# Loading 16 rows of each of eight batches per tile, and scanning during the loads

## The chip, the cores and the metric

The kernel runs on one core of a Trainium2 chip. The metric is device time in microseconds (us), as the median of several executions. The profile is one execution taken by the hardware profiler; its span is about 1.7 us shorter than the measured time (645.1 against 646.76 for the kernel before). "DVE" is VectorE, "PE" TensorE, "ACT" ScalarE, "POOL" GpSimd, "SP" the engine that issues loads. x lies in HBM, the large memory; a load brings it to SBUF, the on-chip memory of 128 partitions; PSUM is where PE leaves its results. "16 engines" in the queue tables are the core's DMA engines, as the page counts them.

## The reference

```
# x: 8 x 2048 x 4096 float32 (268 MB), w: 4096 x 1
proj = (x @ w).squeeze(-1)                      # 8 x 2048
cm = np.maximum.accumulate(proj, axis=1)
is_record = (proj >= cm).astype(np.float32)
return np.cumsum(is_record, axis=1)
```

All of x is read once. The arithmetic is one multiply and one add per element, and then two prefix operations over 2048 values in each of 8 batches.

## The kernel before

x is taken as 16384 rows. Tile t is 128 neighbouring rows, one row (16 KB) to each partition; a load is one uniform step of a row per partition. DVE multiplies by w and sums in one instruction. The last tile is shared between DVE and POOL plus ACT. The results, 128 rows by 128 tiles, are transposed, and then two chains of seven shifted steps compute the prefix maximum and the prefix sum inside blocks of 128, with small matrix work to join the blocks.

```python
x_tiled = x_flat.rearrange("(t v) d -> t v d", v=P)      # P = 128
xpool = ctx.enter_context(tc.tile_pool(name="xpool", bufs=8))
# ... w broadcast to 128 partitions through PE ...
for t in range(NT):                                       # NT = 128
    x_sb = xpool.tile([P, D], FP32)                       # D = 4096
    nc.sync.dma_start(out=x_sb, in_=x_tiled[t])
    # ... (t == NT - 1: POOL multiply and ACT sum of the last 1280 columns) ...
    nc.vector.scalar_tensor_tensor(out=x_sb, in0=x_sb, scalar=1.0, in1=w_bcast,
        op0=mult, op1=mult, accum_out=proj_all[:, t:t + 1])
# ... transpose, two chains of 7 shifted steps, joining of blocks, output ...
```

## Time and profile before

| what | value | where read |
|---|---|---|
| time | 646.76 us (646.76 to 647.03, 3 runs) | executions |
| load rate in the middle | 428 to 435 GB/s | slices of the page |
| load queue | 97.4% of the 16 engines | queue table |
| DVE per tile | starts 4.85 us apart, 4.35 when work is waiting | timeline |
| after the last load | 16.6 us of 645.1 | timeline |

From the page of the kernel before, the busy share of the DMA engines (in tenths) and the rate in 40 equal slices, and the load queue (packets, MB, share of 16 engines):

```profile
DMA  8999999999999999999999999999999999999980
GB/s 350 430 435 429 433 430 432 429 435 428 434 428 433 432 431 431 433 432 430 432 430 434 429 433 429 433 430 432 433 430 434 430 432 429 433 429 435 428 344 4
...
q1 hardware_dynamic: 18578, 268.53, 97.4%
```

The rate is nearly constant from the second slice to the last but two. The timeline of DVE near the end (start, duration, engine, line, operation, and in brackets the idle time before it and what ended it):

```profile
604.27 4.43 DVE L146 SCALAR_TENSOR_TENSOR x_sb<-x_sb,w_bcast 128x4096 f32<-128x4096 f32 x1 [0.42 <-DMA x_sb<-in_x_dram]
...
609.12 4.42 DVE L146 SCALAR_TENSOR_TENSOR x_sb<-x_sb,w_bcast 128x4096 f32<-128x4096 f32 x1 [0.42 <-DMA x_sb<-in_x_dram]
```

Each multiply-reduce waits 0.4 us for its load: starts are 4.85 us apart, and that is the pace of the loads, not of DVE. The group of these instructions on the page (busy us, mean ns, idle before and most of its cause):

```profile
L146 DVE SCALAR_TENSOR_TENSOR x_sb<-x_sb,w_bcast 128x4096 f32<-128x4096 f32 x127 | 560.5, 4425 | 65.7 <-DMA x_sb<-in_x_dram 47.5
```

What this kernel does once the last tile has landed, from its timeline:

```profile
628.56 3.09 DVE L131 SCALAR_TENSOR_TENSOR x_sb<-x_sb,w_bcast 128x2816 f32<-128x2816 f32 x1 [0.41 <-DMA x_sb<-in_x_dram]
628.63 5.75 POOL L120 TENSOR_TENSOR x_sb<-x_sb,w_bcast 128x1280 f32<-128x1280 f32 x1 [624.11 <-DMA x_sb<-in_x_dram]
...
634.42 1.27 ACT L125 ACTIVATE x_sb<-x_sb 128x1280 f32<-128x1280 f32 x1 [615.29 <-POOL x_sb L120]
...
637.01 0.29 DVE L186 TENSOR_TENSOR bufB<-bufA 128x128 f32<-128x128 f32 x1
...
642.34 0.29 DVE L238 TENSOR_SCALAR final<-bufD,ps_ps 128x128 f32<-128x128 f32 x1
642.66 0.35 SPq L243 DMA_DIRECT2D out_dram<-final  x1
```

The last load lands at about 628.5. POOL then takes 5.75 us for its share of the tile, ACT follows, and the chains of shifted steps run from 637 (the first is shown) to 642.6. A faster tail is worth what it takes off these 16.6 us; a faster DVE in the middle is worth nothing.

### The profile page before, as it was taken

To read this page: it belongs to the slowest core of one execution; us is meant where nothing else is said; L and a number is where in the kernel's file an instruction comes from. 1 tells how busy PE (TensorE), PEld (TensorE's weight loads), DVE (VectorE), ACT (ScalarE), POOL (GpSimd) and SP (SyncE) were. 2 spreads that over 40 slices of the span, in tenths; PEclk is the share of its full clock that TensorE was granted. 3 is DMA by queue.
4 is the path that set the end of the run, shared out by engine and by line. 5 is a ranking of instruction groups with operands and counts; after the bars stand their busy time and mean duration, and the time that the engine had idled before them with its cause. 6 is when DMAs were issued, how large, how long until landed. Compare 5 with 4: busy or idle time off the path is not lost.

```text
span 645.1 us, 776 instructions
## 1 busy us (share of the span) xinstructions
PE 15.5 (2%) x20; PEld 6.0 (1%) x20; DVE 570.0 (88%) x279; ACT 6.4 (1%) x5; POOL 9.5 (1%) x21
## 2 busy tenths in 40 slices
PE   7000000000000000000000000000000000000000
PEld 3000000000000000000000000000000000000000
DVE  0899999898998998998989899899899898989984
ACT  1100000000000000000000000000000000000000
POOL 2000000000000000000000000000000000000003
DMA  8999999999999999999999999999999999999980
GB/s 350 430 435 429 433 430 432 429 435 428 434 428 433 432 431 431 433 432 430 432 430 434 429 433 429 433 430 432 433 430 434 430 432 429 433 429 435 428 344 4
DMA packets 18583, 268.57 MB, mean 416 GB/s; under 512 B 2065, under 2 KB 2193, under 8 KB 2193
## 3 DMA queue, kind: packets, MB, share of 16 engines
q1 hardware_dynamic: 18578, 268.53, 97.4%
q14 instruction: 5, 0.04, 0.0%
HBM read 268.45 MB, written 0.07 MB: 416 GB/s over the span
## 4 chain that ended last, share of the span: by engine, by line
DMA 75%; DVE 18%; issue 3%; PE 2%; POOLq 1%; ACT 0%; DVEq 0%; ACTq 0%
DMA x_sb<-in_x_dram 74%; DVE x_sb L146 17%; PE psum_wb L55 2%; POOLq L269 1%; DMA w_bcast<-in_w_dram 0%; ACT w_bcast L62 0%; ACT x_sb L125 0%; DVE bufD L227 0%; DVE bufB L186 0%; DVE bufC L227 0%; DVE bufA L186 0%; PE ps_t L168 0%; DVE bufC L206 0%; DVE bufA L171 0%; DVE final L238 0%
## 5 line engine op out<-in xcount | busy, mean ns | idle before, releaser
L146 DVE SCALAR_TENSOR_TENSOR x_sb<-x_sb,w_bcast 128x4096 f32<-128x4096 f32 x127 | 560.5, 4425 | 65.7 <-DMA x_sb<-in_x_dram 47.5
L168 PE MATMUL ps_t<-identity,proj_all 128*128 128x128 f32 x1 | 0.4, 447 | 618.9 <-DVE proj_all L140 618.9
L120 POOL TENSOR_TENSOR x_sb<-x_sb,w_bcast 128x1280 f32<-128x1280 f32 x1 | 5.8, 5755 | 624.1 <-DMA x_sb<-in_x_dram 624.1
L55 PE MATMUL psum_wb<-w_bcast,ones_70 1*128 1x512 f32 x16 | 14.0, 1064 | 3.2 <-DMA w_bcast<-in_w_dram 3.2
L146 DVE DVE_READ_ACCUMULATOR x_sb<-x_sb,w_bcast 128x1 f32 x127 | 10.5, 83 | 0.0
L125 ACT ACTIVATE x_sb<-x_sb 128x1280 f32<-128x1280 f32 x1 | 1.3, 1269 | 615.3 <-POOL x_sb L120 615.3
L168 PEld LDWEIGHTS ps_t<-identity,proj_all 128*128 128x128 f32 x1 | 0.2, 182 | 620.4 <-issue 620.4
L55 PEld LDWEIGHTS psum_wb<-w_bcast,ones_70 1*128 1x128 f32 x16 | 5.2, 330 | 10.5 <-issue 10.5
L140 DVE TENSOR_TENSOR proj_all<-proj_all,aux_109 128x1 f32<-128x1 f32 x1 | 0.2, 160 | 4.2 <-ACT x_sb L125 4.2
L131 DVE SCALAR_TENSOR_TENSOR x_sb<-x_sb,w_bcast 128x2816 f32<-128x2816 f32 x1 | 3.1, 3093 | 0.4 <-DMA x_sb<-in_x_dram 0.4
L61 ACT COPY w_bcast<-psum_wb 128x2048 f32<-128x2048 f32 x1 | 1.9, 1865 | 6.0 <-PE psum_wb L55 6.0
L62 ACT COPY w_bcast<-psum_wb 128x2048 f32<-128x2048 f32 x1 | 1.9, 1865 | 5.0 <-PE psum_wb L55 5.0
L227 DVE TENSOR_TENSOR bufD<-bufC 128x128 f32<-128x128 f32 x4 | 1.2, 292 | 0.2
L186 DVE TENSOR_TENSOR bufB<-bufA 128x128 f32<-128x128 f32 x4 | 1.2, 291 | 0.2
L61 ACT ACT_TABLE_LOAD x1 | 1.3, 1283 | 3.2 <-DMA w_bcast<-in_w_dram 3.2
L186 DVE TENSOR_TENSOR bufA<-bufB 128x128 f32<-128x128 f32 x3 | 0.9, 292 | 0.2
L227 DVE TENSOR_TENSOR bufC<-bufD 128x128 f32<-128x128 f32 x3 | 0.9, 292 | 0.2
L48 DVE MEMSET ones_70<- 1x128 f32 x1 | 0.2, 165 | 0.9 <-PEq L258 0.9
L171 DVE TENSOR_SCALAR_CACHE_REDUCE bufA<-ps_t 128x128 f32<-128x128 f32 x1 | 0.3, 292 | 0.6 <-PE ps_t L168 0.6
L217 PE MATMUL ps_ps<-blocksum,msum 128*128 128x1 f32 x2 | 0.6, 348 | 2.5 <-DVE bufC L206 2.5
L217 PEld LDWEIGHTS ps_ps<-blocksum,msum 128*128 128x128 f32 x2 | 0.5, 310 | 2.8 <-issue 2.8
L177 PE MATMUL ps_bm<-identity,blockmax 128*128 128x128 f32 x1 | 0.5, 473 | 0.4 <-DVE bufA L171 0.4
(29 smaller groups left out, 6.2 us busy)
## 6 DMA issues: line engine op xcount, KB each, us to landing
x_sb<-in_x_dram SPq DMA_DIRECT2D x128, 2048.0 KB, 34.3
out_dram<-final SPq DMA_DIRECT2D x1, 64.0 KB, 1.5
w_bcast<-in_w_dram SPq DMA_DIRECT2D x1, 16.0 KB
```

Source lines behind the costliest of these rows:

```text
L55: nc.tensor.matmul(out=psum_wb[:, a * 512:(a + 1) * 512], lhsT=ones1, rhs=w_bcast[0:1, a * 512:(a + 1) * 512], start=True, stop=True,)
L61: nc.scalar.copy(out=w_bcast[:, :D // 2], in_=psum_wb[:, :D // 2])
L62: nc.scalar.copy(out=w_bcast[:, D // 2:], in_=psum_wb[:, D // 2:])
L120: nc.gpsimd.tensor_mul(out=x_sb[:, FV:], in0=x_sb[:, FV:], in1=w_bcast[:, FV:],)
L125: nc.scalar.activation(out=x_sb[:, FV:], in_=x_sb[:, FV:], func=mybir.ActivationFunctionType.Copy, accum_out=aux127,)
L131: nc.vector.scalar_tensor_tensor(out=x_sb[:, :FV], in0=x_sb[:, :FV], scalar=1.0, in1=w_bcast[:, :FV], op0=mybir.AluOpType.mult, op1=mybir. ...
L146: nc.vector.scalar_tensor_tensor(out=x_sb, in0=x_sb, scalar=1.0, in1=w_bcast, op0=mybir.AluOpType.mult, op1=mybir.AluOpType.mult, accum_ou ...
L168: nc.tensor.transpose(out=ps_t, in_=proj_all, identity=identity)
L186: nc.vector.tensor_tensor(out=nxt[:, PAD:], in0=cur[:, PAD:], in1=cur[:, PAD - k:W - k], op=mybir.AluOpType.max,)
L217: nc.tensor.matmul(out=ps_ps, lhsT=msum, rhs=blocksum, start=True, stop=True,)
L227: nc.vector.tensor_tensor(out=nxt[:, PAD:], in0=cur[:, PAD:], in1=cur[:, PAD - k:W - k], op=mybir.AluOpType.add,)
L269: with _tile.TileContext(nc) as tc:
```

## The change

Its intent is to bring every batch forward at the same time, 16 rows of each batch per tile, so that the prefix scans can run during the loads, and to have little left at the end. Partition j*8+b holds row j of batch b. For three quarters of the rows a partition takes two neighbouring rows (32 KB). A matmul with 0/1 entries turns 128 results per tile into 8 rows, one for each batch; two scans, chained from group to group, replace the chains of shifted steps. The last tiles are cut into column pieces on DVE.

```diff
-    x_tiled = x_flat.rearrange("(t v) d -> t v d", v=P)
+    NJ = P // B          # 16 rows of each of 8 batches
+    STEP = NJ
+    LONG = 2             # rows per partition, for the first three quarters
+    PIECES = {NT - 4: (0, 4096), NT - 3: (0, 2304, 4096),
+              NT - 2: (0, 2048, 4096), NT - 1: (0, 1920, 4096 - 512, 4096)}
-    xpool = ctx.enter_context(tc.tile_pool(name="xpool", bufs=8))
+    xpool = ctx.enter_context(tc.tile_pool(name="xpool", bufs=5))    # 32 KB each
+    def x_rows(t, r, c0, c1):
+        return bass.AP(
+            tensor=x.tensor,
+            offset=x.offset + t * STEP * D + c0,
+            ap=[[r * D, NJ], [S * D, B], [1, (r - 1) * D + c1 - c0]],
+        )
...
-        nc.sync.dma_start(out=x_sb, in_=x_tiled[t])
+        nc.sync.dma_start(
+            out=x_sb[:, : (r - 1) * D + c1 - c0], in_=x_rows(t, r, c0, c1)
+        )
...
+            nc.scalar.activation(out=dst, in_=is_j, func=ACTF.Copy, scale=acc)
...
+            nc.tensor.matmul(out=ps[:, : n * STEP], lhsT=is_b,
+                             rhs=rhs[:, : n * STEP], start=True, stop=True)
...
+        nc.vector.tensor_tensor_scan(out=cm[:, :N], data0=ps[:, :N], ...)
+        nc.vector.tensor_tensor(out=rec[:, :N], in0=ps[:, :N], in1=cm[:, :N], op=ALU.is_ge)
+        nc.vector.tensor_tensor_scan(out=cnt[:, :N], data0=rec[:, :N], ...)
...
-    # POOL/ACT share of the last tile, transposes, two chains of 7 shifted steps
```

`ap=[[r * D, NJ], [S * D, B], ...]`: the source of a load now has 16 groups of 8 partitions. Two batches lie S*D floats, 32 MiB, apart.

More of the change, by code (lines that the diff above doesn't have):

```diff
@@ L13 @@
 FP32 = mybir.dt.float32
-NEG_BIG = -1.0e30
+ALU = mybir.AluOpType
+ACTF = mybir.ActivationFunctionType
+NEG = -3.0e38
 @with_exitstack
@@ L28 @@
     B, S, D = x.shape
-    R = B * S
-    NT = R // P
-    assert NT == P
-    x_flat = x.flatten_outer_dims()
-    x_tiled = x_flat.rearrange("(t v) d -> t v d", v=P)
-    out_flat = bass.AP(tensor=out.tensor, offset=out.offset,
-                       ap=[[P, NT], [1, P]])
-    const_pool = ctx.enter_context(tc.tile_pool(name="const", bufs=1))
-    xpool = ctx.enter_context(tc.tile_pool(name="xpool", bufs=8))
-    ppool = ctx.enter_context(tc.tile_pool(name="ppool", bufs=1))
+    NJ = P // B
@@ new lines @@
+    STEP = NJ
+    NT = S // STEP
+    LONG = 2
+    LONG_UNTIL = NT - 32
+    PIECES = {
+        NT - 4: (0, 4096),
+        NT - 3: (0, 2304, 4096),
+        NT - 2: (0, 2048, 4096),
+        NT - 1: (0, 1920, 4096 - 512, 4096),
+    }
+    GROUP = 16
+    LASTG = 4
+    const_pool = ctx.enter_context(tc.tile_pool(name="const", bufs=1))
+    xpool = ctx.enter_context(tc.tile_pool(name="xpool", bufs=5))
+    gpool = ctx.enter_context(tc.tile_pool(name="gpool", bufs=2))
+    def x_rows(t, r, c0, c1):
[4 more added lines that the diff above has]
+        )
@@ new lines, with start_load @@
+    loads = []
+    for t in range(0, LONG_UNTIL, LONG):
+        loads.append((t, LONG, 0, D))
+    for t in range(LONG_UNTIL, NT):
+        cuts = PIECES.get(t, (0, D))
+        for c0, c1 in zip(cuts[:-1], cuts[1:]):
+            loads.append((t, 1, c0, c1))
+    def start_load(i):
+        t, r, c0, c1 = loads[i]
+        x_sb = xpool.tile([P, LONG * D], FP32, name="x_sb")
+        nc.sync.dma_start(
+            out=x_sb[:, : (r - 1) * D + c1 - c0], in_=x_rows(t, r, c0, c1)
+        )
+        return x_sb
@@ new lines @@
+    first = [start_load(i) for i in range(2)]
+    w_bcast = const_pool.tile([P, D], FP32)
+    w_row = w_bcast[0:1, :]
+    nc.scalar.dma_start(out=w_row, in_=w.rearrange("d one -> one d"))
+    ones1 = const_pool.tile([1, P], FP32)
+    nc.vector.memset(ones1, 1.0)
+    with tc.tile_pool(name="wbpsum", bufs=1, space=bass.MemoryType.PSUM) as wbpool:
+        psum_wb = wbpool.tile([P, D], FP32)
+        for a in range(D // 512):
+            cols = slice(a * 512, (a + 1) * 512)
+            nc.tensor.matmul(
+                out=psum_wb[:, cols], lhsT=ones1, rhs=w_row[:, cols],
+                start=True, stop=True,
+            )
+        nc.scalar.copy(out=w_bcast[:, : D // 2], in_=psum_wb[:, : D // 2])
+        nc.scalar.copy(out=w_bcast[:, D // 2 :], in_=psum_wb[:, D // 2 :])
@@ L43 @@
+    psum_pool = ctx.enter_context(
+        tc.tile_pool(name="psum", bufs=2, space=bass.MemoryType.PSUM)
+    )
     identity = const_pool.tile([P, P], FP32)
     make_identity(nc, identity)
-    w_bcast = const_pool.tile([P, D], FP32)
-    ones1 = const_pool.tile([1, P], FP32)
-    nc.vector.memset(ones1, 1.0)
-    nc.sync.dma_start(out=w_bcast[0:1, :], in_=w.rearrange("d one -> one d"))
-    with tc.tile_pool(name="wbpsum", bufs=1, space=bass.MemoryType.PSUM) as wbpool:
-        psum_wb = wbpool.tile([P, D], FP32)
-        NCH = D // 512
-        for a in range(NCH):
+    is_b = const_pool.tile([P, B], FP32)
@@ new lines @@
+    is_j = const_pool.tile([P, NJ], FP32)
+    neg = const_pool.tile([B, GROUP * STEP], FP32)
+    zero = const_pool.tile([B, GROUP * STEP], FP32)
+    nc.gpsimd.memset(neg, NEG)
+    nc.gpsimd.memset(zero, 0.0)
+    nc.vector.reduce_sum(
+        out=is_b, in_=identity.rearrange("p (j b) -> p b j", b=B),
+        axis=mybir.AxisListType.X,
+    )
+    nc.vector.reduce_sum(
+        out=is_j, in_=identity.rearrange("p (j b) -> p j b", b=B),
+        axis=mybir.AxisListType.X,
+    )
+    proj = const_pool.tile([P, NT], FP32)
@@ new lines, with scan_group @@
+    parts = const_pool.tile([P, 32], FP32)
+    groups = []
+    t = 0
+    while t < NT:
+        n = GROUP if t + GROUP <= NT - LASTG else (NT - LASTG - t if t < NT - LASTG else LASTG)
+        groups.append((t, n))
+        t += n
+    state = {"cm": None, "cnt": None}
+    def scan_group(t0, n, ps):
+        N = n * STEP
+        cm = gpool.tile([B, GROUP * STEP], FP32, name="cm")
+        rec = gpool.tile([B, GROUP * STEP], FP32, name="rec")
+        cnt = gpool.tile([B, GROUP * STEP], FP32, name="cnt")
+        nc.vector.tensor_tensor_scan(
+            out=cm[:, :N], data0=ps[:, :N], data1=neg[:, :N],
+            initial=NEG if state["cm"] is None else state["cm"],
+            op0=ALU.max, op1=ALU.max,
+        )
+        nc.vector.tensor_tensor(
+            out=rec[:, :N], in0=ps[:, :N], in1=cm[:, :N], op=ALU.is_ge
+        )
+        nc.vector.tensor_tensor_scan(
+            out=cnt[:, :N], data0=rec[:, :N], data1=zero[:, :N],
+            initial=0.0 if state["cnt"] is None else state["cnt"],
+            op0=ALU.add, op1=ALU.add,
+        )
+        state["cm"] = cm[:, N - 1 : N]
+        state["cnt"] = cnt[:, N - 1 : N]
+        eng = nc.sync if t0 + n == NT else nc.scalar
+        eng.dma_start(
+            out=bass.AP(
+                tensor=out.tensor, offset=out.offset + t0 * STEP,
+                ap=[[S, B], [1, N]],
+            ),
+            in_=cnt[:, :N],
+        )
@@ new lines @@
+    pending = None
+    gi = 0
+    rhs = None
+    npart = 0
+    for i, (t, r, c0, c1) in enumerate(loads):
+        x_sb = first[i] if i < 2 else start_load(i)
+        t0, n = groups[gi]
+        if c0 == 0 and t == t0:
+            rhs = gpool.tile([P, GROUP * STEP], FP32, name="rhs")
+        for q in range(r):
+            if c0 == 0 and c1 == D:
+                acc = proj[:, t + q : t + q + 1]
+            else:
+                acc = parts[:, npart : npart + 1]
+                npart += 1
+            xs = x_sb[:, q * D : q * D + c1 - c0]
+            nc.vector.scalar_tensor_tensor(
+                out=xs, in0=xs, scalar=1.0,
+                in1=w_bcast[:, c0:c1], op0=ALU.mult, op1=ALU.mult, accum_out=acc,
+            )
+            base = (t - t0) * STEP
+            dst = rhs[:, base : base + r * STEP].rearrange("p (j q) -> p q j", q=r)[:, q]
+            if c0 == 0:
+                nc.scalar.activation(out=dst, in_=is_j, func=ACTF.Copy, scale=acc)
+            else:
+                nc.vector.scalar_tensor_tensor(
+                    out=dst, in0=is_j, scalar=acc, in1=dst, op0=ALU.mult, op1=ALU.add
+                )
+        if pending is not None and (t + r - 1 >= pending[0] + pending[1] + 1):
+            scan_group(*pending)
+            pending = None
+        if c1 == D and t + r == t0 + n:
+            ps = psum_pool.tile([B, GROUP * STEP], FP32, name="ps")
@@ L55 @@
             nc.tensor.matmul(
-                out=psum_wb[:, a * 512:(a + 1) * 512],
-                lhsT=ones1,
-                rhs=w_bcast[0:1, a * 512:(a + 1) * 512],
+                out=ps[:, : n * STEP], lhsT=is_b, rhs=rhs[:, : n * STEP],
                 start=True, stop=True,
             )
-        nc.scalar.copy(out=w_bcast[:, :D // 2], in_=psum_wb[:, :D // 2])
-        nc.scalar.copy(out=w_bcast[:, D // 2:], in_=psum_wb[:, D // 2:])
-    psum_pool = ctx.enter_context(tc.tile_pool(name="psum", bufs=1, space=bass.MemoryType.PSUM))
@@ L66 @@
-    GB = 16
-    NGB = P // GB
-    blockdiag = const_pool.tile([P, P], FP32)
-    nc.gpsimd.memset(blockdiag, 0.0)
-    nc.gpsimd.affine_select(
-        out=blockdiag, in_=blockdiag,
-        compare_op=mybir.AluOpType.is_gt,
-        fill=1.0, base=1 - GB,
-        pattern=[[-GB, NGB], [0, GB]], channel_multiplier=1,
-    )
-    nc.gpsimd.affine_select(
-        out=blockdiag, in_=blockdiag,
-        compare_op=mybir.AluOpType.is_ge,
-        fill=0.0, base=0,
-        pattern=[[-GB, NGB], [0, GB]], channel_multiplier=1,
-    )
@@ L84 @@
-    strict_lt_col = const_pool.tile([P, P], FP32)
-    nc.gpsimd.memset(strict_lt_col, 1.0)
-    nc.gpsimd.affine_select(
-        out=strict_lt_col, in_=strict_lt_col,
-        compare_op=mybir.AluOpType.is_ge,
-        fill=0.0, base=-1,
-        pattern=[[-1, P]], channel_multiplier=1,
-    )
-    strict_gt_col = const_pool.tile([P, P], FP32)
-    nc.gpsimd.memset(strict_gt_col, 1.0)
-    nc.gpsimd.affine_select(
-        out=strict_gt_col, in_=strict_gt_col,
-        compare_op=mybir.AluOpType.is_ge,
-        fill=0.0, base=-1,
-        pattern=[[1, P]], channel_multiplier=-1,
-    )
@@ L102 @@
-    maxmask = const_pool.tile([P, P], FP32)
-    nc.gpsimd.tensor_mul(out=maxmask, in0=blockdiag, in1=strict_lt_col)
-    nc.gpsimd.tensor_scalar(
-        out=maxmask, in0=maxmask, scalar1=-1.0, scalar2=-NEG_BIG,
-        op0=mybir.AluOpType.add, op1=mybir.AluOpType.mult,
-    )
-    msum = const_pool.tile([P, P], FP32)
-    nc.gpsimd.tensor_mul(out=msum, in0=blockdiag, in1=strict_gt_col)
-    proj_all = const_pool.tile([P, NT], FP32)
-    FV = 2816
-    aux127 = const_pool.tile([P, 1], FP32)
@@ L116 @@
-    for t in range(NT):
-        x_sb = xpool.tile([P, D], FP32)
-        nc.sync.dma_start(out=x_sb, in_=x_tiled[t])
-        if t == NT - 1:
-            nc.gpsimd.tensor_mul(
-                out=x_sb[:, FV:],
-                in0=x_sb[:, FV:],
-                in1=w_bcast[:, FV:],
-            )
-            nc.scalar.activation(
-                out=x_sb[:, FV:],
-                in_=x_sb[:, FV:],
-                func=mybir.ActivationFunctionType.Copy,
-                accum_out=aux127,
-            )
-            nc.vector.scalar_tensor_tensor(
-                out=x_sb[:, :FV],
-                in0=x_sb[:, :FV],
-                scalar=1.0,
-                in1=w_bcast[:, :FV],
-                op0=mybir.AluOpType.mult,
-                op1=mybir.AluOpType.mult,
-                accum_out=proj_all[:, t:t + 1],
-            )
-            nc.vector.tensor_add(
-                out=proj_all[:, t:t + 1],
-                in0=proj_all[:, t:t + 1],
-                in1=aux127,
-            )
-        else:
-            nc.vector.scalar_tensor_tensor(
-                out=x_sb,
-                in0=x_sb,
-                scalar=1.0,
-                in1=w_bcast,
-                op0=mybir.AluOpType.mult,
-                op1=mybir.AluOpType.mult,
-                accum_out=proj_all[:, t:t + 1],
-            )
@@ L156 @@
-    PAD = 64
-    W = PAD + P
-    bufA = ppool.tile([P, W], FP32)
-    bufB = ppool.tile([P, W], FP32)
-    bufC = ppool.tile([P, W], FP32)
-    bufD = ppool.tile([P, W], FP32)
-    nc.gpsimd.memset(bufA[:, :PAD], NEG_BIG)
-    nc.gpsimd.memset(bufB[:, :PAD], NEG_BIG)
-    nc.gpsimd.memset(bufC[:, :PAD], 0.0)
-    nc.gpsimd.memset(bufD[:, :PAD], 0.0)
-    ps_t = psum_pool.tile([P, P], FP32)
-    nc.tensor.transpose(out=ps_t, in_=proj_all, identity=identity)
-    blockmax = const_pool.tile([P, 1], FP32)
@@ L171 @@
-    nc.vector.tensor_scalar(
-        out=bufA[:, PAD:], in0=ps_t, scalar1=1.0, scalar2=None,
-        op0=mybir.AluOpType.mult, op1=mybir.AluOpType.max,
-        accum_out=blockmax,
-    )
-    ps_bm = psum_pool.tile([P, P], FP32)
-    nc.tensor.transpose(
-        out=ps_bm,
-        in_=blockmax.to_broadcast([P, P]),
-        identity=identity,
-    )
-    cur, nxt = bufA, bufB
-    k = 1
-    while k < P:
-        nc.vector.tensor_tensor(
-            out=nxt[:, PAD:],
-            in0=cur[:, PAD:],
-            in1=cur[:, PAD - k:W - k],
-            op=mybir.AluOpType.max,
-        )
-        cur, nxt = nxt, cur
-        k *= 2
@@ L194 @@
-    cm = cur[:, PAD:]
-    masked_bm = ppool.tile([P, P], FP32)
-    prefmax = const_pool.tile([P, 1], FP32)
-    nc.vector.tensor_tensor_reduce(
-        out=masked_bm, in0=ps_bm, in1=maxmask,
-        scale=1.0, scalar=NEG_BIG,
-        op0=mybir.AluOpType.add, op1=mybir.AluOpType.max,
-        accum_out=prefmax,
-    )
-    blocksum = const_pool.tile([P, 1], FP32)
-    nc.vector.scalar_tensor_tensor(
-        out=bufC[:, PAD:],
-        in0=cm,
-        scalar=prefmax,
-        in1=ps_t,
-        op0=mybir.AluOpType.max,
-        op1=mybir.AluOpType.is_le,
-        accum_out=blocksum,
-    )
@@ L216 @@
-    ps_ps = psum_pool.tile([P, 1], FP32)
-    nc.tensor.matmul(
-        out=ps_ps,
-        lhsT=msum,
-        rhs=blocksum,
-        start=True, stop=True,
-    )
-    cur, nxt = bufC, bufD
-    k = 1
-    while k < P:
-        nc.vector.tensor_tensor(
-            out=nxt[:, PAD:],
-            in0=cur[:, PAD:],
-            in1=cur[:, PAD - k:W - k],
-            op=mybir.AluOpType.add,
-        )
-        cur, nxt = nxt, cur
-        k *= 2
-    cs = cur[:, PAD:]
-    final = ppool.tile([P, P], FP32)
@@ L238 @@
-    nc.vector.tensor_scalar(
-        out=final, in0=cs, scalar1=ps_ps, scalar2=None,
-        op0=mybir.AluOpType.add,
-    )
-    nc.sync.dma_start(out=out_flat, in_=final)
+            pending = (t0, n, ps)
+            gi += 1
+    scan_group(*pending)
 _INS = ['x', 'w']
```

## The prediction

> **What bounds the kernel now.** The load stream. The page's slices show 428 to 435 GB/s in all but the first and last two; the queue table gives the load queue 97.4% of the 16 engines. In the timeline VectorE (DVE) multiply-reduce starts are 4.84 to 4.88 us apart, each after a short wait for a load; back to back, behind the late start, 4.35 us. So DVE has 0.49 us of slack per 2 MB tile. After the last landing (about 628.5 us) comes a serial tail to 645.1, 16.6 us: 5.8 POOL multiply, 1.5 ScalarE sum, transposes and fourteen shifted 128x128 steps (636 to 642.6), 2.5 for the output.
>
> **What changes.**
> 1. Loads. Same bytes, 32 KB rows for 96 of 128 tiles. From packet times worked out of the trace (a 16 KB row 611 ns, a 512 B one 27, a semaphore write 9) the fixed part of a row is some ns; halving their number saves about 1.5 us (estimate). The first load no longer queues behind w: 0.4 us. [...]here eight batches lie 32 MiB apart, but the 16 row groups are adjacent, so I expect little loss. No trace here shows it. Last landing: about 626.6.
> 2. DVE gains nine scan groups. [...]against 16 x 0.49 of slack: free, except near the end. The 0/1 matmuls and ScalarE expansions are off the critical path.
> 3. The late start remains (w broadcast on PE, 14 us)[...]. Five 4 MB buffers cover it.
> 4. The tail. POOL, transposes and shift steps go. But the instruction order puts the 192-column scan right after its group's last multiply, so DVE waits there for ScalarE and PE[...]. The last four tiles then cost DVE about 4.35 + 13.4 (seven pieces at 1.04 ns per column + 0.09 us)[...] = 18.9 us, while they land within 14.5. So I expect DVE, not DMA, to end this stage, some 6 us after the last landing, then matmul 0.5[...], output 2.5: about 10 us in place of 16.6.
>
> **Sum.** Stream 1.9 us earlier, tail 6.4 shorter: 8.3 us, nearly all critical. 646.76 - 8.3 = 638.5 us, range 632 to 645. Chances: faster by over 2% 0.17, within 2% 0.75, slower by over 2% 0.08.
>
> **What would show it.** Rate: slices near 432 to 435 GB/s, two-row landings about 9.68 us apart. Tail: in the timeline DVE runs back to back over the pieces, without waits for DMA, from a wait for PE before the 192-column scan; 9 to 11 us from last landing to the end. No wait of the load queue on DVE that leaves the DMA row below 9. If the last pieces wait for DMA instead, DVE was not behind, the tail is 5 us, and the time about 633.
>
> **What would make it wrong.** The new split of rows over DMA engines or the 32 MiB pitch lowers the rate: one per cent is 6 us, a collision far more. Longer rows could gain more than 1.5 us. Scans or semaphore waits on DVE could be longer near the end.

Cut out of it is what no trace of this case shows: in item 1 a statement on distances between rows, in item 2 a speed for scans and two estimates made from it, in item 3 a guess about w, in item 4 three terms that count in scan times. The sums still contain those terms. The first, in item 4, is the wait with scan and comparison; the last four tiles came to 18.9 us on DVE, that is 4.35 + 13.4 and the second; 18.9 less 14.5, plus the first, gives the "some 6 us"; with 0.5, 2.5 and the third the tail came to about 10 us. The stream's 1.9 us are 1.5 + 0.4. The whole came to 8.3 us and so to 638.5 us.

## The result

The changed kernel takes 1282.7 us (median of 4 runs, 1274.2 to 1286.6) against 646.77 us (4 runs). The ratio of the means of the fast runs is 1.98 (95% interval 1.974 to 1.988); ratios here are the mean time of one kernel's fast runs over that of the other's in the same rounds, so not quite the ratio of the quoted medians. The predicted 638.5 us is off by a factor of two.

The same lines of the page of the changed kernel:

```profile
DMA  9999999999999999999999999999999999999997
GB/s 204 208 214 214 214 209 207 211 214 213 210 206 211 214 213 210 203 214 214 208 204 214 213 211 202 214 214 213 210 204 216 220 216 218 216 217 219 215 218 171
...
q1 hardware_dynamic: 12112, 268.44, 99.7%
```

The reader should look at the two rows together. The DMA row reads 9 in all slices but the last, and the queue's share has even risen, from 97.4% to 99.7%; but the rate is 200 to 220 GB/s. The engines are busy all the time and move half as much. The bytes are the same to 0.1%.

The waits of DVE for loads (who waited for what, total us, times, longest us) of the kernel before:

```profile
DVE x_sb L146 <- DMA x_sb<-in_x_dram: 47.5, 106, 1.4
```

The multiply-reduce group on the page of the changed kernel, and then its waits of DVE for loads:

```profile
L172 DVE SCALAR_TENSOR_TENSOR x_sb<-x_sb,w_bcast 128x4096 f32<-128x4096 f32 (+2 forms) x132 | 563.2, 4294 | 676.7 <-DMA x_sb<-in_x_dram 676.7
```

```profile
DVE x_sb L172 <- DMA x_sb<-in_x_dram: 676.7, 83, 21.3
```

An instruction costs what it did (4424 ns for a 128x4096 one, against 4425 before; the group's mean is lower only because it includes the short pieces), and the waits have grown from 47.5 to 676.7 us. In the timeline of DVE a pair of rows takes 8.7 us of work and then DVE waits 11 us:

```profile
202.33 4.43 DVE L172 SCALAR_TENSOR_TENSOR x_sb<-x_sb,w_bcast 128x4096 f32<-128x4096 f32 x1 [11.30 <-DMA x_sb<-in_x_dram]
...
206.68 4.42 DVE L172 SCALAR_TENSOR_TENSOR x_sb<-x_sb,w_bcast 128x4096 f32<-128x4096 f32 x1
...
222.21 4.42 DVE L172 SCALAR_TENSOR_TENSOR x_sb<-x_sb,w_bcast 128x4096 f32<-128x4096 f32 x1 [11.10 <-DMA x_sb<-in_x_dram]
```

Loads of 4 MB are 19.9 us apart, where the prediction had 9.68. Next, two windows of the changed kernel, one with the 32 KB rows and one with the single rows of 16 KB near the end (the window, its length, busy us of PE, PEld, DVE, ACT and POOL with instruction counts, granted clock, DMA share, GB/s):

```profile
0.00:960.00 960.00, 19.09 (x26) 5.60 (x26) 422.87 (x207) 34.05 (x97) 1.20 (x8) 1.00 1.00 211
968.00:1240.00 272.00, 2.85 (x6) 0.31 (x6) 129.29 (x66) 8.91 (x29) 0.00 (x0) 1.00 1.01 217
```

The rate is halved in both, 211 and 217 GB/s, so it isn't the length of the rows. The packet records of the traces agree: the median 16 KB row took 611 ns before and 1245 ns after.

### The profile page after: what moved, and what is told of

Read it like the earlier page. It is cut to its first block, busy times and chain, and to the rows that moved or that the text cites. A ratio compares the mean times of both kernels' runs of the same rounds, so it can differ in the third digit from the quotient of the medians.

```text
span 1272.4 us, 783 instructions
## 1 busy us (share of the span) xinstructions
PE 22.3 (2%) x34; PEld 6.0 (0%) x34; DVE 580.7 (46%) x298; ACT 44.5 (3%) x131; POOL 1.2 (0%) x8
## 2 busy tenths in 40 slices
DMA packets 12247, 268.56 MB, mean 211 GB/s; under 512 B 1425, under 2 KB 1489, under 8 KB 2001
## 3 DMA queue, kind: packets, MB, share of 16 engines
q1 hardware_dynamic: 12112, 268.44, 99.7%
## 4 chain that ended last, share of the span: by engine, by line
another core or an unknown queue 39%; DVE 35%; DMA 25%; PE 0%; issue 0%; ACT 0%; SPq 0%; DVEq 0%
DVE x_sb L172 35%; DMA x_sb<-in_x_dram 25%; PE ps L189 0%; DVE cm L132 0%; DVE cnt L140 0%; DVE rec L137 0%; ACT rhs L179 0%; SPq L72 0%; DVEq L172 0%; DVE rhs L181 0%; DVEq L140 0%
## 5 line engine op out<-in xcount | busy, mean ns | idle before, releaser
L172 DVE SCALAR_TENSOR_TENSOR x_sb<-x_sb,w_bcast 128x4096 f32<-128x4096 f32 (+2 forms) x132 | 563.2, 4294 | 676.7 <-DMA x_sb<-in_x_dram 676.7
L179 ACT ACTIVATE rhs<-is_j,proj 128x16 f32<-128x16 f32 x125 | 38.6, 309 | 1187.3 <-DVE x_sb L172 1156.5
L189 PE MATMUL ps<-rhs,is_b 128*8 128x256 f32 (+2 forms) x18 | 8.3, 566 | 1243.5 <-ACT rhs L179 1210.1
L132 DVE TENSOR_TENSOR_SCAN cm<-ps,cm,neg 8x256 f32<-8x256 f32 (+2 forms) x8 | 5.4, 670 | 9.1 <-PE ps L189 9.1
L140 DVE TENSOR_TENSOR_SCAN cnt<-rec,cnt,zero 8x256 f32<-8x256 f32 (+2 forms) x8 | 5.4, 672 | 0.2
L137 DVE TENSOR_TENSOR rec<-ps,cm 8x256 f32<-8x256 f32 (+2 forms) x9 | 3.4, 382 | 0.3
```

The costliest lines, as they stand in the source:

```text
L132: nc.vector.tensor_tensor_scan(out=cm[:, :N], data0=ps[:, :N], data1=neg[:, :N], initial=NEG if state["cm"] is None else state["cm"], op0= ...
L137: nc.vector.tensor_tensor(out=rec[:, :N], in0=ps[:, :N], in1=cm[:, :N], op=ALU.is_ge)
L140: nc.vector.tensor_tensor_scan(out=cnt[:, :N], data0=rec[:, :N], data1=zero[:, :N], initial=0.0 if state["cnt"] is None else state["cnt"], ...
L172: nc.vector.scalar_tensor_tensor(out=xs, in0=xs, scalar=1.0, in1=w_bcast[:, c0:c1], op0=ALU.mult, op1=ALU.mult, accum_out=acc,)
L179: nc.scalar.activation(out=dst, in_=is_j, func=ACTF.Copy, scale=acc)
L189: nc.tensor.matmul(out=ps[:, : n * STEP], lhsT=is_b, rhs=rhs[:, : n * STEP], start=True, stop=True,)
```

## The experiments

Two theories were on the table.

**P, the pattern and the timing.** The loss comes from how a load deals its rows to partitions and from when these transfers run beside each other, not from where in HBM the rows lie. The figures forecast under P are estimates; what counts is how the runs came out.

**H, HBM.** Rows of different batches lie a power of two apart, 32 MiB, and such a distance costs the rate. No trace showed this beforehand; a figure given for it in the expectation of e2 is cut.

The window of 100 to 500 us of the kernel before and of the changed kernel, for comparison with the runs below:

```profile
100.00:500.00 400.00, 0.00 (x0) 0.00 (x0) 364.39 (x165) 0.00 (x0) 0.00 (x0) 1.00 1.01 431
```

```profile
100.00:500.00 400.00, 3.06 (x6) 0.31 (x6) 181.13 (x89) 12.35 (x40) 0.00 (x0) 1.00 1.00 211
```

### e1_near: the pattern kept, the addresses changed

```diff
-            offset=x.offset + t * STEP * D + c0,
-            ap=[[r * D, NJ], [S * D, B], [1, (r - 1) * D + c1 - c0]],
+            offset=x.offset + t * P * D + c0,
+            ap=[[r * D, NJ], [NJ * r * D, B], [1, (r - 1) * D + c1 - c0]],
```

> [...]Theory H (HBM): the eight batches, 32 MiB apart, collide in HBM. This run keeps the pattern of 16 groups of 8 partitions and brings the eight 'batches' to 256 or 512 KB from each other (wrong result on purpose). P: no change, 1270 to 1290 us, 205 to 220 GB/s. H: back to about 430 GB/s and 635 to 650 us.

Measured: 1296.42 us (one run; wrong result).

```profile
100.00:500.00 400.00, 3.06 (x6) 0.31 (x6) 180.39 (x88) 12.35 (x40) 0.00 (x0) 1.00 1.01 208
```

Bringing the eight groups of rows close together in HBM gained nothing, 208 GB/s against 211 (the time is even 6 us over the range that P gave). The 32 MiB between batches is not the cause. The new distances, 256 and 512 KB, are still powers of two; the next run bears on that.

### e2_pitch: one step for all partitions

```diff
-            offset=x.offset + t * STEP * D + c0,
-            ap=[[r * D, NJ], [S * D, B], [1, (r - 1) * D + c1 - c0]],
+            offset=x.offset + t * D + c0,
+            ap=[[P * D, P], [1, (r - 1) * D + c1 - c0]],
```

> One uniform step of 128 rows (2 MiB) between partitions instead of 16 groups of 8, everything else as in the changed kernel (wrong result on purpose). P: [...]about 430 GB/s and 632 to 645 us. H: all 128 rows of a load lie at a power-of-two distance, so it stays slow, over 800 us[...].

Measured: 659.44 us (one run; wrong result). The first window has 32 KB rows (up to 475 us by the packet records), the second 16 KB rows:

```profile
100.00:500.00 400.00, 5.10 (x10) 0.51 (x10) 370.84 (x182) 25.65 (x83) 0.00 (x0) 1.00 1.00 429
510.00:630.00 120.00, 1.83 (x4) 0.20 (x4) 104.09 (x52) 7.07 (x23) 0.00 (x0) 1.00 1.00 396
```

All 128 rows of a load are 2 MiB apart, and still the full rate is back while rows are 32 KB long. So the fault goes with the pattern of the load. The time missed the upper end of what P expected, 645, for two reasons that the lines show: with 16 KB rows the rate was 396 GB/s, some 8% below the 427 to 430 of e5 in the slices with such rows (that the distance of 2 MiB cost this was not shown, as e2 and e5 differ in more than the distance), and the last two slices of the page, with the short pieces, have 264 and 107. What is left of H is at most an effect of this size, not a factor of two.

### e3_ctrl and e3_phase: the same work, behind two more loads

The control is the changed kernel with one row per partition in all loads, eight buffers, and w loaded to all partitions by one load:

```diff
-    LONG = 2
+    LONG = 1
-    xpool = ctx.enter_context(tc.tile_pool(name="xpool", bufs=5))
+    xpool = ctx.enter_context(tc.tile_pool(name="xpool", bufs=8))
-    # w to one partition, ones-matmul on PE, two ACT copies
+    nc.sync.dma_start(out=w_bcast,
+        in_=bass.AP(tensor=w.tensor, offset=w.offset, ap=[[0, P], [1, D]]))
```

> Control for the next run: changed kernel with one row (16 KB) per partition in all loads, eight buffers of 16 KB, and w loaded to all partitions by one DMA. Correct result. Both theories: still about half rate, 216 GB/s as in the single-row stretch of the changed kernel, 1240 to 1265 us.

Measured: 1252.65 us (one run, correct).

```profile
100.00:500.00 400.00, 3.07 (x6) 0.30 (x6) 187.56 (x92) 12.60 (x41) 0.00 (x0) 1.00 1.01 216
```

The second kernel only puts two loads ahead that nothing reads:

```diff
+    lead_a = const_pool.tile([P, D], FP32)
+    lead_b = const_pool.tile([P, D], FP32)
+    nc.sync.dma_start(out=lead_a[32:80, :],
+        in_=bass.AP(tensor=x.tensor, offset=x.offset, ap=[[D, 12], [S * D, 4], [1, D]]))
+    nc.sync.dma_start(out=lead_b[68:84, :],
+        in_=bass.AP(tensor=x.tensor, offset=x.offset, ap=[[D, 4], [S * D, 4], [1, D]]))
```

The sizes of the two loads, 48 and 16 rows, come from an assumption on the work inside a load, which no trace shows.

> The control with two extra loads ahead ([...]nothing reads them)[...]. P: [...]640 to 700 us[...], with anything under 1000 supporting P. H and every theory in which the addresses or the row lengths cost the time: no gain, 5 to 10 us slower than the control.

Measured: 694.77 us (one run, correct). **A megabyte of loads that nobody needs took 558 us off.** The window of the whole tiles, and that of the column pieces at the end:

```profile
100.00:630.00 530.00, 7.14 (x14) 0.70 (x14) 467.31 (x229) 31.98 (x104) 0.00 (x0) 1.00 1.01 414
640.00:690.00 50.00, 1.18 (x4) 0.22 (x4) 33.83 (x30) 2.19 (x8) 0.00 (x0) 1.00 0.67 161
```

Whole tiles run at 414 GB/s, nearly twice the control's 216. No HBM address, row length or partition of the real loads differs between these two kernels, nor the number of buffers; only what runs ahead of them does. So neither the addresses nor the pattern alone fixes the half rate: the same loads run at 216 or at 414 GB/s. What the two loads change in the course of the transfers was not shown, and other amounts of loads ahead were not tried. The second window, with the column pieces, is a check that was not planned: the rate falls to 161 GB/s. Part of that window is the tail, with a DMA share of 0.67; in the page's slice from 641 to 658 us, where the DMA row still reads 9, the rate is 239 GB/s. So the fall is real, but its cause was not tested.

### e4_quarter: 16 partitions to a load

Each load becomes eight, one for each batch, with partition b*16+j; the 0/1 matrices follow.

```diff
+        for b in range(B):
+            nc.sync.dma_start(out=x_sb[b * NJ : (b + 1) * NJ, :n],
+                in_=bass.AP(tensor=x.tensor, offset=x.offset + b * S * D + t * STEP * D + c0,
+                            ap=[[r * D, NJ], [1, n]]))
```

> Changed kernel with each load cut into eight loads of 16 neighbouring partitions, one for each batch (batch-major partitions, the 0/1 matrices changed to match; correct result). [...]P: [...]a quarter of the full rate, about 108 GB/s and 2300 to 2550 us, although each of these loads is one contiguous block of 256 or 512 KB in HBM. H: [...]faster than the changed kernel, under 800 us.

Measured: 2267.5 us (one run, correct).

```profile
100.00:500.00 400.00, 1.02 (x2) 0.10 (x2) 98.33 (x47) 6.80 (x22) 0.00 (x0) 1.00 1.00 117
```

117 GB/s is 0.27 of the 431 of the kernel before, where the expectation has a quarter, an estimate; the time is just under the expected range. Each of these loads is a contiguous block, and this is the slowest kernel of all: H expected it to be fast. The larger number of loads (eight times as many) is a second difference of this run. It does not account for the loss: the DMA share is 1.00, the 4-byte packets that come with more loads (the page has 10833 packets under 512 B, against 1425) took 24 us per engine in all, and the rows themselves became slow. By the packet records the median 32 KB row took 4444 ns here, 2534 in the changed kernel and 1216 in e5 below.

The eight loads of a tile read the same rows of x as one load of the changed kernel, at 117 GB/s and not 211. What differs is the partitions that the rows go to and the cutting into loads; how that slows the rows was not shown.

### e5_outer32: 32 groups of 4

```diff
-            ap=[[r * D, NJ], [S * D, B], [1, (r - 1) * D + c1 - c0]],
+            ap=[[r * D, 32], [S * D, 4], [1, (r - 1) * D + c1 - c0]],   # batches 0-3, 4-7 in turn
```

> 32 groups of 4 partitions instead of 16 groups of 8 (32 rows of four batches in turn; wrong result on purpose). [...]half rate as in the changed kernel, 1250 to 1300 us. [...]full rate, 635 to 665 us.

The expectation left two outcomes open, half the rate or the full rate.

Measured: 640.3 us (one run; wrong result).

```profile
100.00:500.00 400.00, 5.11 (x10) 0.51 (x10) 370.39 (x182) 25.64 (x83) 0.00 (x0) 1.00 1.00 431
```

This is the full rate, with the same 32 MiB between batches and the same row lengths. What is shown is that a three-part pattern is not slow as such, and that 32 groups of 4 run at 431 GB/s where 16 groups of 8 run at 211; the reason was not shown.

### e6_swdge: loads issued from GpSimd

```diff
-        nc.sync.dma_start(
+        nc.gpsimd.dma_start(
             out=x_sb[:, : (r - 1) * D + c1 - c0], in_=x_rows(t, r, c0, c1)
```

> Changed kernel with all loads of x issued from GpSimd instead of SP; one word changed, correct result. [...]P expects half the rate again, 1260 to 1300 us[...]. H expects no change.

Measured: 1286.67 us (one run, correct), against 1282.7. Who issues the loads made no difference here; the window of 100 to 500 us had 210 GB/s, against 211.

### v1_best: the loads of before with a new tail

The kernel before with prefix scans for the shifted chains, the last 16 tiles in 2, 3 and 4 column pieces, and w loaded on another queue behind the first tile:

```diff
+    PIECED = {t: 2 for t in range(NT - 16, NT - 9)}
+    PIECED |= {t: 3 for t in range(NT - 9, NT - 4)}
+    PIECED |= {t: 4 for t in range(NT - 4, NT)}
...
-    # POOL and ACT share of the last tile; two chains of 7 shifted steps
+    nc.vector.tensor_tensor_scan(out=cm, data0=ps_t, data1=neg, ...)
+    nc.vector.tensor_tensor_scan(out=cs, data0=rec, data1=zero, ...)
```

> A version meant to beat both: the kernel before with its loads of 128 neighbouring rows in one uniform step (full rate), w loaded behind the first tile on another queue, the last 16 tiles in 2, 3 and 4 column pieces on VectorE alone so that its lag behind the loads falls from 4.4 to about 1.2 us, and one prefix scan (0.43 us) in place of each chain of seven shifted steps (2.3 us). Correct result. Expected 637 us, 634 to 641: last landing near 628, about 7.5 us of tail in place of 16.6. P and H agree.

Measured: 644.4 us (644.25 to 644.83), ratio 0.996 to the kernel before (0.994 to 0.998): 7 us short of the estimate.

```profile
GB/s 359 430 432 426 427 431 429 423 429 433 426 426 431 429 424 428 432 428 425 432 429 426 428 430 429 426 429 431 426 426 432 429 426 426 422 420 418 416 409 125
```

The tail did shrink (a scan of 128 columns took 0.42 us, expected 0.43): DVE ends its last piece at 636.4 and the span ends at 643.1, so 6.7 us follow. But by the packet records the last data arrive at 634.7, and in the kernel before at 628.2. The rate in the window of 100 to 500 us was 428 against 431, and it falls to 409 to 422 over the slices with pieces. The second part goes with the shorter rows, though their effect was not tested alone; why the first part is 0.7% lower was not found out.

### v2_fix32 and v3_tail: the change on 32 groups

e5 made right: the loads alternate between batches 0 to 3 and 4 to 7, and two 0/1 matmuls add up in PSUM.

```diff
+        offset=x.offset + (half_of(t, r) * HB * S + row_of(t, r)) * D + c0,   # HB = 4
+        ap=[[r * D, P // HB], [S * D, HB], [1, (r - 1) * D + c1 - c0]],
...
+            for h in range(2):
+                nc.tensor.matmul(out=ps[:, : n * STEP], lhsT=is_b[h],
+                    rhs=rhs[h][:, : n * STEP], start=h == 0, stop=h == 1)
```

> The changed kernel made right with 32 groups of 4 partitions: 32 rows of batches 0 to 3, then 32 rows of batches 4 to 7, two 0/1 matmuls per group of tiles that add up in PSUM; all else as in the change. Correct result. P: full rate, as the run with 32 groups but a wrong result showed, 638 to 643 us, with the tail as there: VectorE back to back over the last pieces. If H held in any form, slower than 660.

Measured: 640.44 us (640.23 to 640.48), ratio 0.990 (0.988 to 0.992), correct. For the tail, see the timeline of DVE of e5_outer32, whose schedule is the same (v2_fix32 differs by 0.2 us in these lines):

```profile
614.52 0.60 DVE L133 TENSOR_TENSOR_SCAN cm<-ps,cm,neg 8x192 f32<-8x192 f32 x1 [1.24 <-PE ps L190]
615.16 0.34 DVE L138 TENSOR_TENSOR rec<-ps,cm 8x192 f32<-8x192 f32 x1
615.43 4.40 DVE L173 SCALAR_TENSOR_TENSOR x_sb<-x_sb,w_bcast 128x4096 f32<-128x4096 f32 x1
...
619.77 2.54 DVE L173 SCALAR_TENSOR_TENSOR x_sb<-x_sb,w_bcast 128x2304 f32<-128x2304 f32 x1
...
633.71 0.69 DVE L173 SCALAR_TENSOR_TENSOR x_sb<-x_sb,w_bcast 128x512 f32<-128x512 f32 x1
```

DVE waits 1.24 us for PE before the 192-column scan and then has no wait for a load until the end; each piece starts when the one before it is done. The last data arrive at 629.2 by the packet records, and DVE ends at 634.8.

The next kernel gives DVE more room there:

```diff
-    PIECES = {NT - 4: (0, 4096), NT - 3: (0, 2304, 4096), ...}
+    PIECES = {t: (0, D // 2, D) for t in range(NT - 6, NT)}
-    LASTG = 4
+    LASTG = 8
-                nc.vector.scalar_tensor_tensor(out=dst, in0=is_j, scalar=acc, in1=dst, ...)
+            # second halves: ACT into rhs_2, added by two more matmuls in PSUM
```

> The run before, with a tail that leaves VectorE more room: the last scan group but one ends eight tiles before the end instead of four, the last six tiles come in halves, and the second halves are added by the matmul in PSUM instead of by VectorE. Correct result. Estimate: VectorE ends about 2.6 us after the last landing instead of 6, then ScalarE 0.4, matmul 0.7, scans 1.2, output 2.5: 636 to 640 us, about 2 us under the run before.

Measured: 638.58 us (638.55 to 638.76), ratio 0.987 (0.986 to 0.989), correct. It is faster than both kernels; against the kernel before by 1.3%, clear of noise. Its timeline at the end:

```profile
629.98 2.29 DVE L182 SCALAR_TENSOR_TENSOR x_sb<-x_sb,w_bcast 128x2048 f32<-128x2048 f32 x1 [0.16 <-DMA x_sb<-in_x_dram]
...
634.72 0.35 SPq L158 DMA_DIRECT2D out_dram<-cnt  x1
```

The last pieces now wait a little (0.16 us) for their loads: DVE is no longer behind, and the last piece ends 2.8 us after the last data at 629.4.

## Why the prediction was wrong

- **The step that failed** is item 1, "the 16 row groups are adjacent, so I expect little loss", and with it the last landing at 626.6 and the 1.9 us for the stream. The stream ended at 1265.8 us by the packet records. The prediction weighed one risk, the distances in HBM, and e1 showed that they cost nothing here. The other, a new split of rows over the DMA engines, stands in its last paragraph as "a collision far more", but was given no number: the chance of slower was 0.08. What the runs put in its place: with 16 groups of 8 partitions the loads ran at half the rate (211 GB/s, 208 with other addresses in e1), with one step for all or 32 groups of 4 at 429 to 431 (before, e2 and e5, with 32 KB rows in the last two), in eight loads of 16 partitions at 117 (e4). Two more loads ahead brought the same loads from 216 to 414 GB/s (e3_phase), so the pattern alone does not fix the rate. The forecasts under P came out in e1 (208 GB/s), in e2 with 32 KB rows (429, forecast 430) and in e3_phase (694.77 us, forecast 640 to 700), and nearly in e4 (117, forecast 108); e5 was left open. That does not prove the cause: no trace shows it.
- **1.5 us from 32 KB rows** (item 1) is not there. Loads of 32 KB rows in e5 ran at 431 GB/s in the window where the 16 KB rows of before run at 431. After 471 us, where e5 has 16 KB rows, it ran at 427 to 430, and the last data came at 629.2, not 626.6.
- **Scans** (item 2) did no harm (e5, with the same scans, ran its loads at 431 GB/s). Measured, a 256-column scan with a chained start took 0.74 us and the 64-column one 0.34. From 64 to 192 columns a scan grew by 0.26 us, 2.0 ns per column, about twice the 1.04 ns of the multiply-reduce.
- **The late start** (item 3) is covered by the buffers, as said: in e5 the second slice is already at 429 GB/s.
- **The tail** (item 4) was right once the rate was: DVE back to back from the 192-column scan (wait for PE 1.24 us, scan 0.60, comparison 0.34), 5.6 us behind the last data (predicted some 6), and 9.3 us to the end of the span (predicted about 10). e5 and v2 at 640.3 and 640.4 lie 1.9 us over the predicted 638.5: the last data came 2.6 us later than predicted, and a tail shorter by somewhat under 1 us made up for part of it.

Open: why loads in 16 groups of 8 partitions are slow, why two loads ahead of them lift the rate, and why eight loads of 16 partitions are slower still (no trace shows it); why the kernel with the two loads ahead ran at 414 and not 431; why v1_best's loads were 0.7% slower in the middle.

## What to carry to other kernels

The outer dimension of a load's source can be part of its speed: in these runs 128 partitions in one uniform step, or 32 groups of 4, had 428 to 432 GB/s in the window of 100 to 500 us (396 later in e2, with rows of 16 KB at 2 MiB from each other), and 16 groups of 8 had 208 to 216 without the two loads ahead. Measure a new pattern alone before building an algorithm on it. When a kernel is bound by loads, read GB/s and not the DMA busy share: here the share rose from 97.4% to 99.7% while the rate halved. Whether addresses or patterns alone make loads slow can be tested by changing only what runs ahead of them: here that took the same loads from 216 to 414 GB/s, though it did not show why.
